# Gate rows of the modulation: stored as one contiguous row per token group, read back in 2 KB packets

## The chip, the cores and the metric

The kernel runs on one core of a Trainium2 chip. The metric is the device time of one execution in microseconds (us). Instructions are named by engine: PE (matrix products), DVE (vector), ACT (activations), POOL (gathers by index) and SP (issues DMAs only). ACT and POOL issue DMAs too.

## The reference, cut to what matters

Two token groups, P (128 context tokens) and S (256 noisy tokens), go through the same two layers. Each group has one conditioning vector, and each layer turns it into six rows of 1024 numbers:

```python
mod = jax.nn.silu(cvec) @ p['ada_w'][l] + p['ada_b'][l]
sh1, sc1, g1, sh2, sc2, g2 = jnp.split(mod[:, None, :], ADA_CHUNKS, axis=-1)
h = rms_norm(x, p['norm1_g'][l]) * (1.0 + sc1) + sh1
mix, kv = token_mixers(h, ...)
x = x + g1 * mix
h = rms_norm(x, p['norm2_g'][l]) * (1.0 + sc2) + sh2
x = x + g2 * peer_ffn(h, ...)
```

`token_mixers` is one input projection, three kinds of mixing and one output projection; `peer_ffn` picks experts by their keys out of 16384 and sums them. The gates g1 and g2 are the same for all tokens of a group: each multiplies a [tokens, 1024] result, so it has to stand in every one of the 128 partitions.

## The kernel before, in words

Each layer has two stages. `chain` does everything up to the choice of experts, for P and S interleaved; its tasks stand in a list with due times, and a scheduler then sets each engine's order with a timing model of its own, so one changed instruction can move others. `experts` follows. P's experts are gathered row by row (256 per layer, POOL issues, DVE multiplies: the tiles `ugt`, `vgt` and `pacc`). S goes densely over all 16384 experts in 128 steps c: SP loads a table block of 512 KB (`raw`), ACT and DVE split it in two (`hi`, `lo`), PE multiplies (`pP`), ACT and DVE make weights (`W`, `whl`), PE sums (`acc`). There are four `raw` buffers, and SP issues its DMAs strictly in order.

The six rows are made in twelve pieces of 512 columns by `ada_chunk`: PE multiplies four weight loads (`w`) into four 32-row groups of the bank `pada`, DVE adds the bias, and the tile `row` then holds, in partition 32q + r, columns 128q to 128q + 127 of group r (r = 0 is P, r = 1 is S; the other 30 rows of each 32 carry nothing). Shifts and scales are transposed on PE. Gates (`which` 2 and 5) go to HBM, into `grow`: SP stores the whole `row` tile, 128 rows of 512 bytes, once for each piece, eight times in all: four for layer 0 and four for layer 1, all of them while layer 0's `chain` runs (L200).

The gate comes back through `gate_half`: ACT issues a DMA that reads the group's four 512-byte rows of one half, 16 KB apart in `grow`, and writes them to all 128 partitions. All partitions read the same four rows. There are sixteen such reads: eight into `wo`, one for each half, group and layer, just before the output projection's result is multiplied by g1 (`wout`), and eight into two free `G` tiles in the dense loop (`finish`, c = FIN), where ACT first loads x of the group, then the two halves of g2.

The profile gives one line, L82, to everything that PE, DVE, ACT and POOL do, since a helper records it; so the rows are told apart by tile. SP's DMAs keep their lines: L314 loads `w`, L1014 loads `raw`, L200 stores `grow`.

Of the kernel before, what the change touches and what calls it, by code (L numbers as in the profile page):

```python
# [9 lines left out]
F32 = mybir.dt.float32  # L10
# [9 lines left out]
D = 1024  # L20
# [78 lines left out]
def trunk_kernel(ctx, tc, xin, silu_c, wts, adab, ccol, crow, finalg, rope, ohc, io2, skt,  # L99
                 sgut, lkT, lv, ut, ug, vg, y, ck_d, cv_d, ck_g, cv_g):  # L100
    nc = tc.nc
    V, A, TE, SY, GP = nc.vector, nc.scalar, nc.tensor, nc.sync, nc.gpsimd
# [6 lines left out]
    dpool = ctx.enter_context(tc.tile_pool(name="dpool", bufs=2, space=bass.MemoryType.DRAM))  # L109

    V, TE, A, GP = Follow(V), Follow(TE), Follow(A), Follow(GP)
# [3 lines left out]
    def bank(name, st=None):  # L115
        if st is not None and name + st.name in cur["tags"]:
            name += st.name
        tag, n = cur["tags"][name]
        return cur["psum"].tile([128, 512], F32, tag=tag, name=name, bufs=n)
# [45 lines left out]
    def transposes(cols, st=None):  # L165
        pt = bank("pt", st)
        for i, c in enumerate(cols):
            TE.transpose(pt[:, i * 128:(i + 1) * 128], c, ident)
        return pt
# [4 lines left out]
    def new_layer(l):  # L174
        L = Layer()
        L.l, L.have = l, set()
        L.lam_init = 0.8 - 0.6 * math.exp(-0.3 * l)
        L.modT = sp.tile([128, 4, KC, 2], F32, name="modT")
        L.cc = sp.tile([128, 20], F32, name="cc")
        A.dma_start(L.cc, ccol[l])  # L180
        L.grow = dpool.tile([2, 2, 128, 128], F32, name="grow")
        return L

    def ada_chunk(L, j, pieces):
        which, half = divmod(j, 2)
        L.have.add(j)
        ab = sm.tile([128, 128], F32, name="ab", bufs=2)
        A.dma_start(ab, adab[L.l, j])
        ps = bank("pada")
        k = 0  # L190
        for w in pieces:
            for kk in range(w.shape[1]):
                for q in range(4):
                    TE.matmul(ps[32 * q:32 * q + 32, 0:128], sT[:, k, :], w[:, kk, q * 128:(q + 1) * 128],
                              start=(k == 0), stop=(k == KC - 1), tile_position=(0, 32 * q))
                k += 1
        row = sm.tile([128, 128], F32, name="row", bufs=2)
        V.tensor_tensor(row, ps[:, 0:128], ab, op=ALU.add)
        if which in (2, 5):
            SY.dma_start(L.grow[which // 3, half], row)  # L200
            return
        pt = transposes([row])
        pv = pt[:, 0:128].rearrange("p (q r) -> p q r", r=32)[:, :, 0:2]
        m = {0: 0, 1: 1, 3: 2, 4: 3}[which]
        dst = L.modT[:, m, half * 4:(half + 1) * 4, :]
        if m % 2:
            g = L.cc[:, (m // 2) * 8 + half * 4:(m // 2) * 8 + half * 4 + 4]
            V.scalar_tensor_tensor(dst, pv, 1.0, g[:, :, None].to_broadcast([128, 4, 2]), op0=ALU.add, op1=ALU.mult)
        else:
            V.tensor_copy(dst, pv)  # L210

    def gate_half(L, which, half, row, gb):
        src = L.grow[which, half].rearrange("(q r) c -> q r c", r=32)[:, row, :]
        A.dma_start(gb.rearrange("p (q c) -> p q c", q=4), src[None].to_broadcast([128, 4, 128]))

    def gate_rows(L, which, row, gb):
        src = L.grow[which].rearrange("h (q r) c -> h q r c", r=32)[:, :, row, :]
        A.dma_start(gb.rearrange("p (h q c) -> p h q c", h=2, q=4), src[None].to_broadcast([128, 2, 4, 128]))


    class Retrieval:
# [64 lines left out]
    def chain(L, early_ada, Ln, R0):  # L286
        l = L.l
        with ExitStack() as es:
# [78 lines left out]
            def ada(M, js, cost, free=12):  # L367
                for j in js:
                    while j >= free and not cur["queried"]:
                        yield 3  # L370

                    ada_chunk(M, j, kpieces(j, P, M.l, S if M.l == 0 and j in (1, 3) else P))
                    yield cost
# [263 lines left out]
            def wout(st, blocks):  # L637
                for b in blocks:
                    load_x(st, b)
                yield from need(4, 5)  # L640
                for half in range(2):
                    hs = slice(half * 512, (half + 1) * 512)
                    pss = mm_tok(16 + half, [(st.mixT, b) for b in blocks], st)
                    g = s512(st, "wo")
                    gate_half(L, 0, half, st.row, g)
                    yield CW * st.nb
                    for b, ps in zip(blocks, pss):
                        t = s512(st, "wo")
                        V.tensor_tensor(t, ps, g, op=ALU.mult)
                        V.tensor_tensor(st.xs[b][:, hs], st.xs[b][:, hs], t, op=ALU.add)  # L650
                for b in blocks:
                    xd = dpool.tile([128, D], F32, name=f"x1{st.name}{b}")
                    SY.dma_start(xd, st.xs[b])
                    st.x[b] = xd
# [177 lines left out]
            def head(st):  # L832
                if not st.past and R0 is not None and LEFT:
                    while R0.n < NSLOT + R0.LAG:
                        yield 1.0
                    for half in range(2):
                        hs = slice(half * 512, (half + 1) * 512)
                        gb = s512(st, "gb")
                        gate_half(R0.L, 1, half, st.row, gb)
                        V.tensor_tensor(gb, R0.acc[:, hs], gb, op=ALU.mult)  # L840
                        V.tensor_tensor(st.xs[0][:, hs], st.xs[0][:, hs], gb, op=ALU.add)
                    xd = dpool.tile([128, D], F32, name="x2p")
                    SY.dma_start(xd, st.xs[0])
                    st.x[0] = xd
                elif st.next:
                    st.xs, st.next = st.next, {}
                else:
                    st.xs = {}
                    for b in range(st.nb):
                        load_x(st, b)  # L850
                if not st.past:
                    alloc_mix(st)
                    if st.hT is not None:
                        return
                hp = pp if st.past else tp
                st.hT = hp.tile([128, KC, st.T], F32, name=f"hT{st.name}")
                yield from normed_T(st, 0, st.hT, range(st.nb))
# [139 lines left out]
    def experts(L, R, Ln):  # L997
        l = L.l
        last = l == DEPTH - 1
        with ExitStack() as es:  # L1000
# [161 lines left out]
            def finish(c):  # L1162
                late_p = not last and LEFT
                if c == FIN[l]:
                    sp, sq = (g_tile(i).rearrange("p a t -> p (a t)").rearrange("p (n d) -> p n d", d=D) for i in (8, 9))
                    for i, n in enumerate(("xs0", "xs1", "gs")):
                        fin[n] = [sq[:, i, hs] for hs in halves]
                    fin["xp0"] = [sp[:, 0, hs] for hs in halves]
                    fin["gp"] = [sp[:, 1, hs] for hs in halves]
                    fin["fg"], fin["out"] = sp[:, 2], [sp[:, 3], sp[:, 0]]  # L1170
                    for st in (P, S):
                        if st is P and late_p:
                            continue
                        for b in range(st.nb):
                            for hs, t in zip(halves, fin[f"x{st.name}{b}"]):
                                A.dma_start(t, st.x[b][:, hs])
                        for half, t in enumerate(fin["g" + st.name]):
                            gate_half(L, 1, half, st.row, t)
                    if last:
                        A.dma_start(fin["fg"], finalg.to_broadcast([128, D]))  # L1180
# [66 lines left out]
            dense_loop()  # L1247

    L, R = new_layer(0), None
    for l in range(DEPTH):  # L1250
        Ln = new_layer(l + 1) if l + 1 < DEPTH else None
        R = chain(L, l == 0, Ln, R)
        R.L = L
        experts(L, R, Ln)
        L = Ln
# [86 lines left out]
```

## Time and profile before

| | |
|---|---|
| three runs | 2392.46, 2394.32, 2396.28 us; median 2394.32 |
| profiled execution | 2388.71 us, span 2386.9 us, granted PE clock 0.968 |
| busy share of the span | PE 93%, DVE 78%, ACT 37%, POOL 32% |
| DMA | 681.25 MB in 201998 packets, mean 285 GB/s |
| gate stores | 8, from 116.3 to 487.2 us |
| gate reads into `wo` | 8, from 128.6 to 1478.9 us |
| gate reads into `G` | 8, from 863.1 to 2094.9 us |

Layer 0's `chain` ends near 487 us and its dense loop near 1238 us; layer 1's end near 1622 and 2371 us. The share of busy time is an average over these four stretches. What one DMA costs has to be read in the few microseconds around it: who waits there, and how busy the 16 DMA engines are. A row of a stretch ("windows") gives busy time and instructions by engine, then the granted PE clock, the mean busy share of the 16 DMA engines and GB/s.

### The profile page before, as it was taken

The numbers are of one execution on the slowest core, as the hardware profiler recorded it, in microseconds if no ns is written. First come the engines' busy times: TensorE is split into PE (matmuls) and PEld (weight loads), VectorE is DVE, ScalarE is ACT, GpSimd is POOL, SyncE is SP. The second block draws the span as 40 slices with busy tenths as digits, with TensorE's granted clock in tenths as the row PEclk, the third lists the DMA queues.
The fourth block names the chain that finished last, engine by engine and source line by source line (L and its number), as shares of the span: only waits on it lengthen the run. The fifth ranks groups of instructions, "written<-read, shape, count | busy, mean of one in ns | idle before, by whom it ended". The sixth has DMA issues, their size and how long they took to land.

```text
span 2386.9 us, 38803 instructions
## 1 busy us (share of the span) xinstructions
PE 2218.8 (93%) x14466; PEld 1726.2 (72%) x14466; DVE 1860.0 (78%) x3795; ACT 894.4 (37%) x1848; POOL 755.0 (32%) x558
## 2 busy tenths in 40 slices
PE   6999879889999989999999998797999999999997
PEld 4446537676898768899974464586689877889996
DVE  1234668987999959899962466899889996999996
ACT  2224311143444334444442343114344343444443
POOL 0000043103544425455400002400345443545540
PEclk9998989999999999999999999899999999999999
DMA  8665699738998869999976424942899887999994
GB/s 331 211 221 175 215 356 360 275 111 293 369 376 319 287 224 400 366 375 383 367 257 203 130 89 147 356 138 90 291 356 388 336 285 260 394 386 383 380 374 161
DMA packets 201998, 681.25 MB, mean 285 GB/s; under 512 B 22225, under 2 KB 37201, under 8 KB 201809
## 3 DMA queue, kind: packets, MB, share of 16 engines
q1 hardware_dynamic: 112448, 397.66, 45.8%
q0 software_dynamic: 74160, 270.04, 30.7%
q10 hardware_dynamic: 15200, 11.07, 1.9%
q8 instruction: 114, 1.87, 0.3%
q14 instruction: 76, 0.61, 0.1%
HBM read 671.08 MB, written 7.60 MB: 284 GB/s over the span
## 4 chain that ended last, share of the span: by engine, by line
PE 71%; DVE 15%; DMA 9%; ACT 2%; issue 2%; ACTq 0%; POOL 0%; DVEq 0%; SPq 0%; POOLq 0%
PE acc L82 27%; PE pP L82 23%; PE mm L82 10%; DMA raw<-in_vg 3%; DMA w<-in_wts 3%; PE pt L82 3%; PE sc L82 2%; PE pG L82 2%; DVE ugt L82 2%; DVE si L82 2%; DVE pacc L82 2%; DVE lo L82 2%; DMA ugt<-in_ug,ei 1%; PE pq L82 1%; PE pg L82 1%
## 5 line engine op out<-in xcount | busy, mean ns | idle before, releaser
L82 POOL DMA_INDIRECT ugt<-in_ug,ei x256 | 360.8, 1409 | 975.9 <-DVE ugt L82 811.7
L82 DVE TENSOR_TENSOR lo<-raw,hi 128x1024 fp32r<-128x1024 f32 x418 | 504.9, 1220 | 108.5 <-ACT hi L82 90.4
L82 ACT ACTIVATE hi<-raw 128x1024 fp32r<-128x1024 f32 x418 | 435.6, 1057 | 343.4 <-DMA raw<-in_vg 179.4
L82 PE MATMUL acc<-hi,whl 128*128 128x512 f32 x1680 | 479.5, 400 | 19.3 <-ACT whl L82 11.2
L82 PE MATMUL pP<-hh,lo 128*128 128x256 f32 x1664 | 465.9, 280 | 8.8 <-DVE lo L82 8.7
L82 PE MATMUL pP<-hh,hi 128*128 128x256 f32 x1664 | 469.1, 282 | 1.5 <-ACT hi L82 1.5
L82 PE MATMUL pP<-hl,hi 128*128 128x256 f32 x1664 | 463.1, 278 | 0.0
L82 POOL DMA_INDIRECT vgt<-in_vg,ei x256 | 362.5, 1416 | 167.7 <-DVE pacc L82 73.2
L82 PEld LDWEIGHTS acc<-hi,whl 128*128 128x128 f32 x1680 | 313.2, 191 | 88.4 <-ACT whl L82 11.8
L82 DVE SCALAR_TENSOR_TENSOR ugt<-ugt,h 128x1024 f32<-128x1024 f32 x256 | 311.7, 1218 | 28.6 <-DMA ugt<-in_ug,ei 26.9
L82 DVE SCALAR_TENSOR_TENSOR pacc<-vgt,gz,pacc 128x1024 f32<-128x1024 f32 x254 | 324.9, 1279 | 3.9 <-DMA vgt<-in_vg,ei 3.5
L82 PEld LDWEIGHTS pP<-hh,lo 128*128 128x128 f32 x1664 | 312.6, 188 | 19.4 <-DVE lo L82 12.1
L82 PEld LDWEIGHTS pP<-hh,hi 128*128 128x128 f32 x1664 | 314.4, 189 | 10.3 <-issue 3.3
L82 PEld LDWEIGHTS pP<-hl,hi 128*128 128x128 f32 x1664 | 312.7, 188 | 3.0 <-issue 0.5
L82 PE MATMUL acc<-lo,whl 128*128 128x512 f32 x840 | 264.4, 398 | 0.1
L82 PEld LDWEIGHTS acc<-lo,whl 128*128 128x128 f32 x840 | 155.8, 191 | 31.5 <-DVE lo L82 0.7
L82 ACT ACTIVATE W<-pP 128x512 f32<-128x512 f32 x104 | 62.1, 597 | 300.0 <-PE pP L82 249.6
L82 POOL TENSOR_TENSOR rstd<-rstd,mhalf 128x1 f32<-128x1 f32 (+3 forms) x34 | 29.1, 861 | 434.1 <-DVE rstd L82 434.1
L82 ACT ACTIVATE G<-pG 128x128 f32<-128x128 f32 x512 | 94.4, 301 | 76.5 <-PE pG L82 75.5
L82 PE MATMUL mm<-w,hTs 128*128 128x512 f32 x256 | 117.6, 610 | 1.9 <-DMA w<-in_wts 1.8
L82 DVE TENSOR_TENSOR o<-ohio,i12d 128x2048 f16<-128x2048 f16 (+1 forms) x128 | 117.9, 952 | 0.8 <-DMA ohio<-in_io 0.7
L82 PE MATMUL mm<-hTs,w 128*128 128x256 f32 x512 | 117.9, 387 | 0.0
(248 smaller groups left out, 2716.2 us busy)
## 6 DMA issues: line engine op xcount, KB each, us to landing
raw<-in_vg SPq DMA_DIRECT2D x256, 512.0 KB
w<-in_wts SPq DMA_DIRECT2D x224, 512.0 KB
raw<-in_ut SPq DMA_DIRECT2D x224, 512.0 KB
w<-in_ut SPq DMA_DIRECT2D x32, 512.0 KB
ugt<-in_ug,ei POOLq DMA_INDIRECT x256
vgt<-in_vg,ei POOLq DMA_INDIRECT x256
x<-in_xin SPq DMA_DIRECT2D x5, 512.0 KB
wo<-grow ACTq DMA_DIRECT2D x8, 256.0 KB
```

What stands on the lines that cost most here:

```text
L82: self.last = f(*a, **k)
```

## The change

`grow` becomes one row of 1024 numbers for each gate and group. Each piece is stored by two DMAs, one for each group, that take four rows of 512 bytes each out of `row` and put them side by side. A half of a gate is then one piece of 2 KB, and a read is 128 packets of 2 KB where it was 512 packets of 512 bytes; it writes the same 256 KB. `gate_rows`, which nothing called, goes.

```diff
-        L.grow = dpool.tile([2, 2, 128, 128], F32, name="grow")
+        L.grow = dpool.tile([2, 2, D], F32, name="grow")
...
         if which in (2, 5):
-            SY.dma_start(L.grow[which // 3, half], row)
+            for r in range(2):
+                SY.dma_start(L.grow[which // 3, r, half * 512:half * 512 + 512].rearrange("(q c) -> q c", q=4),
+                             row.rearrange("(q r) c -> q r c", r=32)[:, r, :])
             return
...
     def gate_half(L, which, half, row, gb):
-        src = L.grow[which, half].rearrange("(q r) c -> q r c", r=32)[:, row, :]
-        A.dma_start(gb.rearrange("p (q c) -> p q c", q=4), src[None].to_broadcast([128, 4, 128]))
-
-    def gate_rows(L, which, row, gb):
-        src = L.grow[which].rearrange("h (q r) c -> h q r c", r=32)[:, :, row, :]
-        A.dma_start(gb.rearrange("p (h q c) -> p h q c", h=2, q=4), src[None].to_broadcast([128, 2, 4, 128]))
+        src = L.grow[which, row:row + 1, half * 512:half * 512 + 512]
+        A.dma_start(gb, src.to_broadcast([128, 512]))
```

The engines' instructions are the same in kind and number but for SP's eight more stores. The scheduler moves some near the end of layer 0's `chain`. On SP, at the end of that stage, before (the last `w` loads, a gate store, the small table `ohio` that the dense loop starts with, the first `raw` loads, the last gate store):

```order
L314 DMA w<-in_wts 128x1024 x5
L200 DMA grow<-row 128x128
L1004 DMA ohio<-in_io 128x128
L1014 DMA raw<-in_ut 128x1024 x4
L200 DMA grow<-row 128x128
```

The same place now:

```order
L312 DMA w<-in_wts 128x1024 x6
L201 DMA grow<-row 4x128 x2
L1002 DMA ohio<-in_io 128x128
L1012 DMA raw<-in_ut 128x1024 x4
L201 DMA grow<-row 4x128 x2
```

One more store stands ahead of `ohio`, and one more `w` load ahead of the store.

On PE at the same place, before (`pt<-ident,eo` turns S's chosen experts round for the dense loop, once for each block of 128 tokens, twice a block; `mm<-hTs,w` and `pada` are work for the dense loop and for layer 1 that fills gaps):

```order
L82 MATMUL pada<-w,sT 32x128 x13
L82 MATMUL pt<-ident,eo 128x128
L82 MATMUL pada<-w,sT 32x128 x11
L82 MATMUL mm<-hTs,w 128x256 x10
L82 MATMUL pada<-w,sT 32x128
L82 MATMUL pt<-ident,eo 128x128
L82 MATMUL pt<-ident,gate 128x128
```

And now:

```order
L82 MATMUL pada<-w,sT 32x128 x14
L82 MATMUL pt<-ident,eo 128x128
L82 MATMUL pada<-w,sT 32x128 x2
L82 MATMUL mm<-hTs,w 128x256 x3
L82 MATMUL pada<-w,sT 32x128 x8
L82 MATMUL mm<-hTs,w 128x256 x3
L82 MATMUL pada<-w,sT 32x128 x2
L82 MATMUL pt<-ident,eo 128x128
L82 MATMUL pt<-ident,gate 128x128
```

Between the last two `eo` transposes stood ten `mm` products and now stand six; the other four come after.

## The prediction

> **What bounds the kernel.** I read the page first, for the share of the engines and of the chain that ended last, then the DMA queues.
>
> ```profile
> span 2386.9 us, 38803 instructions
> PE 71%; DVE 15%; DMA 9%; ACT 2%; issue 2%; ACTq 0%; POOL 0%; DVEq 0%; SPq 0%; POOLq 0%
> q10 hardware_dynamic: 15200, 11.07, 1.9%
> L82 ACTq DMA_DIRECT2D wo<-grow x8: 366/384/1355, 128.6 to 1478.9; - x8
> L82 ACTq DMA_DIRECT2D G<-grow x8: 377/575/976, 863.1 to 2094.9; - x8
> ```
>
> PE bounds most of the span, and DMA holds 9% of the chain, some 215 us. ACT's own queue (q10), on which all sixteen gate reads run, keeps the DMA engines busy for 1.9% of the span. By the averages the change touches nothing. The last two rows (issue time, minimum/median/maximum in ns) say where the reads are, so I took the stretch around each of them. Here is one that runs almost alone, then the only other read of one row into all partitions that does (the parameter row `cr`, packets of 2304 bytes, at the start of layer 1), then a plain load (`ab`, 512-byte packets, a different address in every partition):
>
> ```profile
> DMA packets 422, 0.21 MB, mean 43 GB/s; under 512 B 3, under 2 KB 422, under 8 KB 422
> q10 hardware_dynamic: 422, 0.21, 27.7%
> ```
>
> ```profile
> DMA packets 35, 0.08 MB, mean 115 GB/s; under 512 B 0, under 2 KB 0, under 8 KB 35
> q10 hardware_dynamic: 35, 0.08, 28.8%
> ```
>
> ```profile
> DMA packets 136, 0.06 MB, mean 155 GB/s; under 512 B 15, under 2 KB 136, under 8 KB 136
> ```
>
> The stretches are 1336 to 1341, 1235.5 to 1236.2 and 467.4 to 467.8 us. A gate read gets 422 packets through in 5 us, 84 a microsecond and 43 GB/s, with the engines busy 28% of the time: nothing else competes, and still 512 packets need 6.1 us. The plain load moves packets of the same size at 155 GB/s. So it isn't the engines that are slow, it is reading the same few rows again and again. With longer packets from one row, `cr` gets 115 GB/s.
>
> What that does to others stands in the windows around the reads that fall among weight loads or gathers:
>
> ```profile
> 132.00:138.00 6.00, 6.00 (x69) 3.42 (x67) 2.35 (x12) 1.43 (x4) 0.70 (x1) 1.00 0.45 102
> 181.00:187.00 6.00, 6.00 (x15) 2.65 (x15) 2.29 (x4) 0.00 (x0) 0.00 (x0) 1.00 0.75 65
> 238.00:245.00 7.00, 6.13 (x55) 4.92 (x54) 4.33 (x25) 2.44 (x7) 1.01 (x1) 1.00 0.38 91
> 319.00:332.00 13.00, 11.34 (x57) 4.17 (x56) 10.40 (x19) 0.20 (x1) 6.61 (x6) 1.00 1.03 375
> 865.00:879.00 14.00, 12.50 (x64) 8.46 (x63) 1.24 (x2) 0.35 (x1) 0.00 (x0) 1.00 0.42 109
> 968.00:988.00 20.00, 18.46 (x110) 15.77 (x109) 16.71 (x21) 9.24 (x12) 9.72 (x7) 1.00 0.99 349
> 1480.00:1488.00 8.00, 8.00 (x20) 3.42 (x18) 4.92 (x8) 0.00 (x0) 5.23 (x5) 1.00 0.42 108
> 2006.00:2012.00 6.00, 6.00 (x20) 2.99 (x18) 2.42 (x2) 1.06 (x1) 0.00 (x0) 1.00 0.65 156
> 2100.00:2104.00 4.00, 4.00 (x37) 3.96 (x36) 3.66 (x5) 1.14 (x2) 1.80 (x2) 1.00 0.90 297
> ```
>
> The last column should be near 400 where loads are waiting (375 at 319); it falls to 65 to 109. All queues crawl while a gate read is under way. The chain of waits (start, us, what) carries a load there each time (the row at 467 is for later), and the timeline (start, us, engine, instruction, in brackets the idle time before it and who ended it) shows PE or DVE idle behind it:
>
> ```profile
> 130.11 11.03 DMA w<-in_wts
> 187.91 7.22 DMA w<-in_wts
> 237.34 10.46 DMA w<-in_wts
> 467.11 4.22 DVE eq L82 x9
> 865.04 14.79 DMA raw<-in_vg
> 1484.97 15.35 DMA ugt<-in_ug,ei
> 2007.22 8.84 DMA raw<-in_vg
> 2100.51 12.40 DMA raw<-in_vg
> ```
>
> ```profile
> 141.28 8.80 PE L82 MATMUL mm<-w,hTs 128*128 128x512 f32 x16 [1.82 <-DMA w<-in_wts]
> 191.45 0.64 PE L82 MATMUL pada<-w,sT 128*32 128x128 f32 x16 [3.57 <-DMA w<-in_wts]
> 247.85 1.08 PE L82 MATMUL pada<-w,sT 128*32 128x128 f32 x16 [3.72 <-DMA w<-in_wts]
> 877.22 0.28 PE L82 MATMUL pP<-hl,hi 128*128 128x256 f32 x1
> 882.19 0.58 ACT L82 ACTIVATE W<-pP 128x512 f32<-128x512 f32 x1
> 884.72 1.22 PE L82 MATMUL acc<-hi,whl 128*128 128x512 f32 x2 [7.22 <-ACT whl L82]
> 2020.94 1.22 PE L82 MATMUL acc<-hi,whl 128*128 128x512 f32 x2 [3.83 <-ACT whl L82]
> 1489.69 1.23 DVE L82 SCALAR_TENSOR_TENSOR ugt<-ugt,h 128x1024 f32<-128x1024 f32 x1 [4.70 <-DMA ugt<-in_ug,ei]
> ```
>
> **What a 2 KB read costs.** No row shows it. From below: if the packet is what counts, 128 packets at 84 a microsecond take 1.5 us. From above: if bytes from one place count, 256 KB at 43 GB/s take 6.1 us as before. I take `cr`'s 115 GB/s, 2.3 us, because its packets are nearest in size and also read by all partitions. A read then blocks the queues 3.8 us less, a pair 7.6 us.
>
> **The sum, stall by stall.** Every gain is capped by the idle time that PE or DVE has there.
> - 128.6 us: PE idles 1.82, so 1.8. 179.4: 3.57 at 191 and more in the products just after it, so the whole 3.8. 236.6: capped at 3.7.
> - 316.2: the engines are full (1.03), so only the packets' own time counts. 27.7% of 16 engines for 5 us over 422 packets is 53 ns a packet, 1.7 us for 512 packets spread over 16 engines; `cr` had 28.8% for 0.7 us over 35, 92 ns, 0.7 us for 128. The difference, 1.0, contains waiting and lies on no engine's path as such: 0 to 1.0, I take 0.2.
> - 863 (two reads): the `raw` load lands 7.6 earlier, but the products ahead of it keep PE until 877.5, and from the start of W on ACT to `acc` it is 2.5 (882.19 to 884.72); 884.7 becomes 880.0, gain 4.7. 962 (two): engines at 0.99, so 0.5 of 0 to 2.0.
> - 1335, 1374, 1424: as at 1336, no other load is in flight, nobody waits: 0. These three could be worth something only if the gate itself were late for DVE.
> - 1478.9: at a share of 0.42 the eight us lose 4.6 us of DMA time, the new read 1.6 (2.3 us at 0.28); the gathers are asked for a little late, so 2.5.
> - 2000 (two): PE idles 3.83, of which 2.5 are again the steps from W on: 1.3. 2094 (two): share 0.90, and ACT's issues (up to 976 ns) stand ahead of the next `hi`: 1.5.
>
> That makes 20.0. How much of it stays? SP issues a load when a buffer comes free, so what is late behind a stall is late by as much, and shifts with it; but between 342 and 472 us most pieces of the chain are DVE's (the one at 467 is the longest), and DVE also limits the loop from 885 to 1000. I keep 0.8: 16.0 (0.6 and 1 are the ends, 12.0 and 20.0).
>
> **The stores and the moved instructions.** SP issues eight DMAs more, and DVE's first step of the dense loop waits behind two of them:
>
> ```profile
> L200 SPq DMA_DIRECT2D grow<-row x8: 320/403/692, 116.3 to 487.2; - x8
> 474.01 5.78 PE L82 MATMUL mm<-hTs,w 128*128 128x256 f32 x20
> 480.54 0.42 DVE L82 CAST i<-pt 128x256 f16<-128x256 f32 x1 [5.42 <-PE pt L82]
> 481.97 4.71 DMA ohio<-in_io
> ```
>
> One store more ahead of `ohio`: +0.4 (403 ns), and the one after it delays `raw` loads that have four buffers. The others fall between `w` loads; if SP finds its buffers taken, as it mostly does there, they cost nothing, and 7 times 0.4 is their most. A store's 8 packets for 128 of the same size can only shorten it. On PE, ten `mm` products (twenty passes, 5.78 us) stood between the two `eo` transposes while DVE idled 5.42 for them; six stand there now, so 4 times 0.58: 2.3 less. The other moved rows are fillers under DVE's chain: 0, up to 2 either way.
>
> Sum: 16.0 + 2.3 - 0.4 = 17.9. The profiled execution took 2388.71 us (span 2386.9), which gives 2370.8; the median of the runs, 2394.32, is 5.6 above that execution, so I forecast 2376 for the median.
>
> **The rivals.**
> - Nothing happens to the reads. The Trainium skill, "DMA: Bandwidth & Descriptors", section Specifications, gives 512 bytes as the smallest transfer at line rate; by it packets of 512 bytes are long enough and 2 KB buys nothing. The trace at 1336 doesn't bear the rule out for a row that everyone reads (43 GB/s), but the same would follow if one place in HBM yields 43 GB/s at any packet size. Then 16 reads at 6.1 us remain, and 2.3 - 0.4 is all: 2392. Against it stands `cr`, an input at another place. Chance 0.15.
> - The reads get short, but DVE takes the time back: the first three gains (9.3) vanish between 342 and 472, that at 863 (4.7) in the loop up to 1000. 6.0 + 1.9 are left: 2386. For it: DVE is busy for 16.71 of the 20 us at 968; against it: for 1.24 of the 14 at 865, behind the load. Chance 0.15.
> - Slower, through SP: six of the eight second stores wait, in the new program, for an earlier DMA's semaphore. If that DMA is a `w` load still in flight, SP stands and so do all loads behind. The longest such wait so far is 3.4 us:
>
> ```profile
> SPq L314 <- DMA w<-in_wts: 21.1, 10, 3.4
> ```
>
>  Four stores before 270 us at 3.4 + 0.4 make 15.2; with unshortened reads, less 2.3, the result is 2407. From 5 us a store it would outweigh even the gain. Chance 0.07.
>
> **How the numbers follow.** The forecast has 0.63, at 2364 to 2383 by itself (2364: reads of 1.5 us, every stall's idle time gone and all kept; 2383: little more than half kept and no gain from the moved products). A change of 0.2%, 4.8 us, is about the least that a measurement of this kernel tells from none. Faster is the forecast and the second rival, less a little: 0.77; within 0.2% 0.16; slower 0.07. The range, 2362 to 2392, leaves out the SP rival and the far side of the first one.
>
> **What would show it.** Right: the read at 1336 takes 2 to 3 us from first to last packet, at 90 to 170 GB/s; the windows above no longer fall under 150 GB/s for 6 us; the loads at 130, 237 and 865 are 3 to 8 us shorter; DVE's wait of 5.42 is near 3. The first rival: that read still moves 43 GB/s. The second: the stalls are gone and DVE's gaps between 342 and 472 or at 885 to 1000 are wider. The third: SP waits for DMAs just ahead of L201. The forecast is wrong if a stall had a second cause behind the read, such as loads that SP issued late.

## The result and the profile after

The changed kernel takes 2358.76 us (median of 4 runs, 2354.8 to 2361.86), the kernel before, run beside it, 2395.03 (2392.46 to 2396.28). The ratio is 0.9849, 95% interval 0.9832 to 0.9866. The gain is 36.3 us between medians; 2376 was forecast, and the range ended at 2362. The profiled execution took 2361.86 us, 26.9 less than the one of before. One execution of `only_wo` below ran at a granted clock of 0.744 and took 2815 us; its ratio leaves it out. From the page of the profile after, the span, the chain that ended last, and ACT's own queue:

```profile
span 2360.1 us, 38816 instructions
PE 72%; DVE 14%; DMA 7%; issue 3%; ACT 2%; POOL 1%; ACTq 0%; POOLq 0%; DVEq 0%; SPq 0%
q10 hardware_dynamic: 9056, 11.07, 1.5%
```

DMA's share of the chain fell from 9% to 7% (in a second profile of each, from 12% to 6%), and q10 moves the same bytes in 6144 packets fewer (16 reads by 384). The same kernel's windows, at the places of six of the nine rows of before (busy time and instructions by engine, clock, DMA share, GB/s):

```profile
131.50:137.50 6.00, 6.00 (x69) 3.43 (x67) 2.36 (x13) 1.43 (x4) 0.70 (x1) 1.00 1.00 332
177.00:183.00 6.00, 6.00 (x14) 2.65 (x15) 2.44 (x5) 0.00 (x0) 0.00 (x0) 1.00 0.58 170
228.50:235.50 7.00, 7.00 (x74) 5.89 (x74) 4.24 (x24) 2.44 (x7) 1.01 (x1) 1.00 0.73 218
851.00:865.00 14.00, 14.00 (x72) 9.87 (x71) 8.63 (x12) 5.84 (x8) 3.16 (x3) 1.00 0.75 256
1455.50:1463.50 8.00, 8.00 (x20) 3.56 (x19) 6.88 (x11) 0.00 (x0) 5.86 (x5) 1.00 0.96 326
1984.00:1990.00 6.00, 6.00 (x19) 2.89 (x18) 1.57 (x2) 1.37 (x2) 0.00 (x0) 1.00 0.88 313
```

Where before the last column fell to 65 to 156, it now stays at 170 or above; at the other three places it was 297 to 375 and is 404 to 408. The read that runs alone, now at 1309.6 (the DMA view of 1310.6 to 1312.4):

```profile
DMA packets 135, 0.26 MB, mean 142 GB/s; under 512 B 13, under 2 KB 13, under 8 KB 134
q10 hardware_dynamic: 134, 0.25, 57.1%
```

From its first packet to its last it takes 2.0 us where it took 6.2. All of that looks like the forecast. The reason given for it, longer packets, was wrong, as the next runs show.

### The profile page after: what moved, and what is told of

The parts are those of the page before. It is cut to its first block, busy times and chain, and to the rows that moved or that the text cites. A ratio compares the mean times of both kernels' runs of the same rounds, so it can differ in the third digit from the quotient of the medians.

```text
span 2360.1 us, 38816 instructions
## 1 busy us (share of the span) xinstructions
PE 2211.2 (94%) x14466; PEld 1722.7 (73%) x14466; DVE 1861.4 (79%) x3795; ACT 890.6 (38%) x1848; POOL 754.2 (32%) x558
## 4 chain that ended last, share of the span: by engine, by line
PE 72%; DVE 14%; DMA 7%; issue 3%; ACT 2%; POOL 1%; ACTq 0%; POOLq 0%; DVEq 0%; SPq 0%
PE acc L82 27%; PE pP L82 24%; PE mm L82 9%; PE pt L82 3%; DMA ugt<-in_ug,ei 2%; PE pq L82 2%; DMA w<-in_wts 2%; PE pG L82 2%; DVE ugt L82 2%; DMA raw<-in_vg 2%; PE sc L82 2%; DVE pacc L82 1%; PE pada L82 1%; DVE si L82 1%; DVE lo L82 1%
```

## The experiments

Each run's ratio is against the kernel before on the same chip.

### Which part of the change does it: the packets, or the stores and the moved instructions?

`reads_512` is the changed kernel with short packets, with the same instructions in the same order on every engine:

```diff
-L.grow = dpool.tile([2, 2, D], ...)
+L.grow = dpool.tile([2, 2, 8, 256], ...)          # pieces of 512 bytes, 1 KB apart
-SY.dma_start(L.grow[which // 3, r, half * 512:half * 512 + 512].rearrange(...), ...)
+SY.dma_start(L.grow[which // 3, r, half * 4:half * 4 + 4, 0:128], ...)
-src = L.grow[which, row:row + 1, half * 512:half * 512 + 512]
+src = L.grow[which, row, half * 4:half * 4 + 4, 0:128]      # 4 packets of 512 bytes
...
```

> The changed kernel, but a gate read is again 512 packets of 512 bytes (the four pieces of a row lie 1 KB apart in HBM). The two stores, and the order of the instructions on every engine, are those of the changed kernel. Theory A (the packets' length is the whole change): nothing is left of the gain, 2395 us within 5, and the read that runs alone near 1310 takes 6 us. Rival B (about half of the 36 us comes from the moved instructions and the stores, since my sum for the reads was 16): 2377.

Measured: 2358.31 us, ratio 0.9857 (0.9836 to 0.9878). Both theories missed. The long packets are worth nothing: with 512 packets of 512 bytes, 1 KB apart instead of 16 KB, the lone read (window 1308.5 to 1310.4) runs as fast as with 2 KB.

```profile
DMA packets 517, 0.27 MB, mean 140 GB/s; under 512 B 14, under 2 KB 516, under 8 KB 516
q10 hardware_dynamic: 516, 0.26, 46.0%
```

`reads_2k_only` is the other half: before's order, one store of 128 rows a piece, and 2 KB reads. Against the kernel before (the read, left out here, is that of the changed kernel):

```diff
-L.grow = dpool.tile([2, 2, 128, 128], ...)
+L.grow = dpool.tile([2, 32, D], ...)
-SY.dma_start(L.grow[which // 3, half], row)
+SY.dma_start(L.grow[which // 3, :, half * 512:half * 512 + 512].rearrange("r (q c) -> q r c", q=4), row)
...
```

> The kernel before, with its one store of 128 rows a piece and its order on every engine, but the store puts a group's pieces side by side, so that a read is 128 packets of 2 KB. Theory A: the whole gain, 2359 us within 5. Rival B: only the reads' part, 2377. If A holds here and in the run with short packets, the two stores and the moved instructions are worth less than 5 us together.

Measured: 2360.22 us, 0.9855 (0.983 to 0.988). The whole gain comes without the second stores and without any moved instruction: together these are worth nothing that can be told from zero.

`reads_spread` keeps the stores, the order and the packets' number and length of before, but lets each partition read a stored row of its own, four times; the rows lie 512 bytes apart:

```diff
-src = L.grow[which, half].rearrange("(q r) c -> q r c", r=32)[:, row, :]     # 4 rows for all
+src = L.grow[which, half]                                # row p for partition p, four times
...
```

> The kernel before, same order, same stores, same 512 packets of 512 bytes in a read, but each partition reads one row of its own of the 128 stored ones, four times (so the gate's values are others). Theory C (one row that everyone reads is slow): the read alone takes about 256 KB / 155 GB/s = 1.7 us, and the time is that of the changed kernel or a little less, 2350 to 2362. Rival D (the number of packets is what costs): 6 us, and 2395 as before.

Measured: 2360.43 us, 0.9862 (0.9842 to 0.9882); theory C holds. The same 512 packets, alone at 1308.2 to 1309.2:

```profile
DMA packets 509, 0.25 MB, mean 253 GB/s; under 512 B 15, under 2 KB 509, under 8 KB 509
```

So it is neither the length nor the number of packets, it is where they read. And a read of 1.1 to 1.4 us makes the kernel no faster, as far as these intervals tell, than one of 2.0.

### How far apart may the pieces lie?

Two kernels of DMAs only. The first:

> A kernel of DMAs only; it computes nothing of the reference. Reads of 128 partitions from HBM on ACT's queue, one after the other, from 1, 4, 16 and 128 different rows and in packets of 512 bytes to 4 KB; first alone, twice, then under a stream of 512 KB loads that SP issues. Theory C: the time goes by packets that hit the same row, about 64 to 84 a microsecond: 4 rows with 512 packets 6 us, 1 row with 512 packets 6 us or more, 1 KB packets 3 to 4 us, 2 KB 2 us, 4 KB from one row about 2 to 3 us though it is twice the bytes; 16 and 128 rows near 200 GB/s or more, 1.3 us for 256 KB. Rival D: 512 packets take 6 us from 128 rows too, and 128 packets 2 us from any number of rows. Under the stream: with one row the loads fall below 150 GB/s for as long as the read takes; with 128 rows they stay over 300.

Its windows, each from a read's first packet to its last (the last column is GB/s): four times the same 512 bytes; 128 rows, 4 KB apart, in 512-byte packets; one, 16 and 128 rows in 2 KB packets; one row in 4 KB packets.

```profile
55.48:61.99 6.51, 0.00 (x0) 0.00 (x0) 1.00 0.21 40
63.40:65.29 1.89, 0.00 (x0) 0.00 (x0) 1.00 0.48 138
70.35:72.10 1.75, 0.00 (x0) 0.00 (x0) 1.00 0.45 150
78.38:79.53 1.15, 0.00 (x0) 0.00 (x0) 1.00 0.62 228
81.16:82.45 1.29, 0.00 (x0) 0.00 (x0) 1.00 0.63 203
84.04:86.08 2.04, 0.00 (x0) 0.00 (x0) 1.00 0.67 255
```

One place of 512 bytes gives 40 GB/s, a row of 2 KB 150, a row of 4 KB 255. Rival D is out: 512 packets from 128 rows take 1.89 us. Theory C holds in kind but not in all: the four rows 128 KB apart took 3.0 and 3.9 us instead of 6. Nor do the bytes that a read spreads over set the rate alone: 128 rows 4 KB apart give 138 in 512-byte packets and 203 in 2 KB ones, where 16 rows give 228, and four rows of 2 KB, not shown, gave 86 to 96. The part under a stream of loads says nothing, since SP's loads waited for the reads there (SP's waits: total, times, longest):

```profile
SPq L54 <- DMA gb<-h: 118.3, 7, 70.1
```

The second scans the distance, from three starts:

> A kernel of DMAs only; it computes nothing of the reference. 128 partitions read 256 KB each time from HBM: one place of 512 bytes, 1 KB, 2 KB again and again, then four pieces of 512 bytes at distances from 640 bytes to 128 KB; all from three different starts. Theory E: 41 GB/s for one place of 512 bytes, about 80 for 1 KB, 130 to 150 for 2 KB; four pieces give 120 to 150 at most distances, and 42 at 16 KB and at some of its multiples, at every start. Rival F: the rate falls with the distance, and is low at all of 8 KB and more.

The third start: one place of 512 bytes, 1 KB, 2 KB; then four pieces of 512 bytes at 640 bytes, 1, 2, 4, 8, 16, 20, 32, 64 and 128 KB from each other.

```profile
144.98:151.37 6.39, 0.00 (x0) 0.00 (x0) 1.00 0.22 41
152.70:155.80 3.10, 0.00 (x0) 0.00 (x0) 1.00 0.36 84
157.08:158.83 1.75, 0.00 (x0) 0.00 (x0) 1.00 0.44 149
160.23:162.02 1.79, 0.00 (x0) 0.00 (x0) 1.00 0.53 146
163.40:165.21 1.81, 0.00 (x0) 0.00 (x0) 1.00 0.49 145
166.56:168.31 1.75, 0.00 (x0) 0.00 (x0) 1.00 0.52 150
169.66:173.29 3.63, 0.00 (x0) 0.00 (x0) 1.00 0.45 72
174.68:180.57 5.89, 0.00 (x0) 0.00 (x0) 1.00 0.25 44
182.10:188.01 5.91, 0.00 (x0) 0.00 (x0) 1.00 0.25 44
189.35:192.45 3.10, 0.00 (x0) 0.00 (x0) 1.00 0.35 85
193.80:199.69 5.89, 0.00 (x0) 0.00 (x0) 1.00 0.19 45
201.12:205.61 4.49, 0.00 (x0) 0.00 (x0) 1.00 0.32 58
206.98:210.02 3.04, 0.00 (x0) 0.00 (x0) 1.00 0.36 86
```

The three starts agree within a fifth. 41, 84, 149: about 40 GB/s for each place of 512 bytes that the pieces cover. Up to 2 KB apart four pieces lie in four places, 4 and 20 KB apart in two, 8, 16 and 32 KB apart in one. That reads as a period of 8 KB; at 64 and 128 KB it doesn't fit (58 and 86 where it says 44), so it isn't the whole address rule. Theory E holds for 16 KB and misses 4, 8 and 20 KB; rival F is wrong, since 20 KB is faster than 8 and 16.

`pitch_20k` and `pitch_16k5` put that into the kernel before, with one number changed:

```diff
-L.grow = dpool.tile([2, 2, 128, 128], ...)
+L.grow = dpool.tile([2, 2, 128, 160], ...)[:, :, :, 0:128]     # pitch_20k
+L.grow = dpool.tile([2, 2, 128, 132], ...)[:, :, :, 0:128]     # pitch_16k5
```

> The kernel before with one number changed: a stored row of grow takes 640 bytes of room, so the four pieces of a group lie 20 KB apart instead of 16 KB. Packets, stores and order on all engines are those of before. Theory E (rows 16 KB apart fall into one place of HBM, which yields 42 GB/s, and other distances don't): the read alone takes about 2 us, and the whole gain comes, 2360 us within 5. Rival F (pieces must lie near each other, within a KB or so): the read stays near 6 us, 2393. Rival G (there are few places, and 20 KB hits two of them): 3 to 4 us for the read, 2368 to 2380.

> The kernel before with one number changed: a stored row of grow takes 528 bytes of room instead of 512, so the four pieces of a group lie 16.5 KB apart instead of 16 KB. Packets, stores and order are those of before. If places repeat every 8 KB and are 512 bytes long (as the scan of distances reads: 2 KB apart 150 GB/s, 4 KB apart 72, 8 and 16 KB apart 44), the pieces now fall 0, 512, 1024 and 1536 bytes into that period, four places: the read alone takes 1.8 to 2.2 us, the load behind the pair at 863 is waited for 5 us instead of 14.6, and the time is 2359 within 5. If distances over 16 KB are bad as such, the time is 2370, as at 20 KB, or more.

20 KB: 2369.95 us, 0.9900 (0.9886 to 0.9914), rival G's number. 16.5 KB: 2362.08 us, 0.9856 (0.9817 to 0.9894), the whole gain from sixteen bytes a row. The three reads that run alone take 1.8 to 3.4 us in the first and 1.9 to 2.6, a little over the 1.8 to 2.2 expected, in the second. One stall shows the dose: ACT's first wait for the `raw` load behind the read pair in layer 0's loop, on ACT's timeline (in brackets the idle time), in before, `pitch_20k`, `pitch_16k5`, `reads_512` and after:

```profile
879.94 1.06 ACT L82 ACTIVATE hi<-raw 128x1024 fp32r<-128x1024 f32 x1 [14.58 <-DMA raw<-in_vg]
```

```profile
859.24 1.06 ACT L82 ACTIVATE hi<-raw 128x1024 fp32r<-128x1024 f32 x1 [9.09 <-DMA raw<-in_vg]
```

```profile
855.03 1.06 ACT L82 ACTIVATE hi<-raw 128x1024 fp32r<-128x1024 f32 x1 [6.29 <-DMA raw<-in_vg]
```

```profile
853.38 1.06 ACT L82 ACTIVATE hi<-raw 128x1024 fp32r<-128x1024 f32 x1 [4.97 <-DMA raw<-in_vg]
```

```profile
855.81 1.06 ACT L82 ACTIVATE hi<-raw 128x1024 fp32r<-128x1024 f32 x1 [4.75 <-DMA raw<-in_vg]
```

### Does a slow read really hold up other queues?

`dma_block` has seven loads at once on one queue and one read on the other.

> A kernel of DMAs and small vector steps; it computes nothing of the reference. Twelve phases, six kinds twice: seven loads of 512 KB issued at once on SP's queue, and on ACT's queue no read, or one read of 256 KB into all partitions: four pieces of 512 bytes 16 KB apart, 4 KB apart, 1 KB apart, one piece of 2 KB, and 128 rows of 2 KB. Theory C (a read from one place starves the loads): a phase without a read moves 3.67 MB at about 410 GB/s, 9 us; with a read from 128 rows 0.64 us more, which is its bytes; with four pieces in one place 5 us more or above; 4 KB apart 2 to 3, 1 KB apart and 2 KB 1 to 2. Rival H (the slow read only waits by itself, and in the kernel it is the waits for its end that cost): the loads land as early with it as without, give or take 0.7 us.

Windows from the loads' first packet to their last, second round: no read; pieces 16, 4 and 1 KB apart; one piece of 2 KB; 128 rows.

```profile
90.17:100.89 10.72, 1.00 (x6) 0.00 (x0) 1.00 0.89 342
102.93:117.78 14.85, 1.00 (x6) 0.00 (x0) 1.00 0.77 265
120.10:132.61 12.51, 1.00 (x6) 0.00 (x0) 1.00 0.83 314
134.68:146.37 11.69, 1.00 (x6) 0.00 (x0) 1.00 0.91 336
148.47:160.28 11.81, 1.01 (x6) 0.00 (x0) 1.00 0.95 333
162.39:173.08 10.69, 1.00 (x6) 0.00 (x0) 1.00 0.97 368
```

The loads end 4.1 us later beside the read from one place (the slow read), 1.8 beside two places, 1.0 and 1.1 beside four, not at all beside 128 rows. Theory C holds in kind, a little below its numbers, and rival H is out: the read takes the time from the loads themselves. SP's timeline shows a part of it: handing a load to the queue takes SP 0.3 to 0.5 us mostly, but 3.47 once beside the slow read and 1.31 once beside two places. In the kernel before, SP's third `raw` load behind the read pair at 863 took 2.76 us to hand over, where after the change it took 0.33.

### Which reads carry the gain?

`only_wo` and `only_g` are `reads_2k_only` for one gate, with the other stored and read as before:

```diff
+if which // 3 == 0:      # only_wo; == 1 in only_g
+    ... store and read as in reads_2k_only
+else:
+    ... store and read as before
```

> The kernel before with its order, but only the gate of the mixers (the eight reads into wo) has its pieces side by side and 2 KB reads; the gate of the experts is as before. From the traces of before and after, stall by stall: up to 285 us 16.3, at 1479 4.7, so 21 gained, of which the loop may take back 4: 2372 to 2376. Rival, by the prediction's sum: 12.0 for these reads, times 0.8: 2383.

> The kernel before with its order, but only the gate of the experts (the eight reads into G) has its pieces side by side and 2 KB reads. From the traces of before and after: 9.9 at 863, 3.1 at 985, 4.4 at 2000, about 1.5 at 2094, so 19: 2374. Rival, by the prediction's sum: 8.0, times 0.8: 2387. If the two parts add, the gains of this run and of the one with wo alone make 33 to 36 together; if DVE takes gains back between the stages, they make more than the whole.

Ratios 0.9928 (0.9909 to 0.9947) and 0.9907 (0.989 to 0.9924), which is 17 us (13 to 22) and 22 us (18 to 26) of 2394. The two parts add up to the whole within their intervals. The forecasts from the traces, 2372 to 2376 and 2374, lie inside (2372 at the edge); those from the prediction's sum, 2383 and 2387, outside.

### Is there more to be had?

`one_read` is `reads_2k_only` with both halves of a gate in one read of 4 KB packets in the loop:

```diff
-for half, t in enumerate(fin["g" + st.name]):
-    gate_half(L, 1, half, st.row, t)
+A.dma_start(t, L.grow[1, st.row:st.row + 1, :].to_broadcast([128, D]))     # t: both halves
```

> The kernel with one store of 128 rows a piece and 2 KB reads, but in the loop the two halves of a gate are read at once, 128 packets of 4 KB: four reads instead of eight into G, and four issues of 0.5 us less on ACT. If reads still cost, each pair is about 1.6 us shorter (2.2 instead of 3.8 us) and the loop gains up to 6 us: 2353. If they have stopped to cost, as the run with every partition reading its own row says (1.3 us a read, and no faster than 2.0), 2359 within 4.

2356.72 us, 0.9845 (0.982 to 0.9871): no difference from the changed kernel that can be told. The interval, 2350 to 2363 us, holds both numbers expected, so this run doesn't decide whether the reads still cost; that they cost nothing that can be told rests on `reads_spread`.

### How much do two executions of one kernel differ?

> The kernel before once more, for a second profile. The profile that the prediction was made from took 2388.71 us, below all other executions seen by then. If that was chance, this one lies at 2390 to 2397, and the difference of 6 or so stands at the stalls behind gate reads if those scatter (the read pair at 863, the loads at 128, 179, 237), elsewhere if they don't.

> The changed kernel once more, for a second profile: 2355 to 2362. Held against the second profile of before, the difference is 32 to 38 us, where the first two profiles differ by 26.9.

2391.78 and 2363.74 us, 28.0 apart. The first lies where chance would put it; the second and the difference miss what was expected. The profiled pairs differ by 27 and 28, the medians by 36 and, over all runs of both here, by about 34. The first profile of before lies low among its kernel's runs and both of after lie high, by chance as far as the runs tell: a difference of two profiles is good to some 8 us here (36 less 28).

## Why the prediction was wrong, step by step

To size the stalls I compared starts of the same PE and DVE instructions, stretch by stretch, over all profiles: executions with slow reads at that place (before twice, and the part run that leaves it alone) against those with fast reads (after twice, `reads_512`, `reads_2k_only`, `reads_spread` and the other part run). The last row leaves out both part runs. The time of a stretch less that in the first execution of before, in us (negative is shorter), and the gain, slow less fast:

```
stretch     read          slow reads       fast reads         gain   forecast
                          mean (spread)    mean (spread)
 120- 150   128.6       -1.2 (-2.0..0.0)  -3.6 (-3.6..-3.6)   2.3     1.8
 150- 210   179.4       -1.9 (-4.3..0.0)  -2.9 (-3.6..-2.3)   1.0     3.8
 210- 285   236.6       -3.2 (-5.9..0.0)  -8.9 (-9.6..-6.7)   5.7     3.7
 285- 485   316.2       -0.4 (-1.7..0.4)  -0.4 (-1.9..0.6)   -0.1     0.2
 858- 895   863 pair    -0.2 (-0.8..0.3)  -9.6 (-9.6..-9.5)   9.4     4.7
 895- 995   962 pair     1.9 ( 0.0..2.9)  -0.3 (-1.4..0.3)    2.2     0.5
1230-1470   three alone  1.0 ( 0.0..2.9)   0.9 (-0.3..2.5)    0.1     0
1470-1490   1478.9       0.3 ( 0.0..0.6)  -3.2 (-3.6..-2.7)   3.5     2.5
1995-2090   2000 pair    0.1 (-0.2..0.4)  -3.9 (-5.4..-2.7)   4.0     1.3
2090-2160   2094 pair    2.6 ( 0.0..6.5)  -0.7 (-1.5..0.9)    3.3     1.5
1490-1560   (no read)    0.6 ( 0.0..1.2)   4.2 ( 1.0..5.5)   -3.6
```

The reads' stretches make 31.4 where 20.0 was forecast. The `wo` reads make 12.5, against 12.0, but that is luck: 2.8 too much at 179.4 stands against 2.0 too little at 236.6 and 1.0 at 1478.9. The loop's four pairs make 18.9, against 8.0. So in the forecast of 17.9 for the profile the loop's reads were 10.9 short, the factor 0.8 took 4.0 more, and the moved products less the store gave 1.9 that did not come.

- **The step that failed: "every gain is capped by the idle time that PE or DVE has there".** It priced the loop's four pairs at 8.0 us, and they gained 18.9; the forecast's best case, 2364, stood under the same cap. At 863 the 4.7 us that are missing are two things: 2.5 us of idle time were taken off without need (the next point), and 2.2 us are what idle time does to PE's clock, which the cap leaves out. At 2000, 2.7 are missing, and the same 2.5 are nearly all of it. At 962 and 2094 the forecast's 0.5 and 1.5 were choices; 2.2 and 3.3 came, and no run separates the causes there. For the clock, before, the windows behind the late product at 247.9, then just ahead of that at 884.7, from it on, and 4 us later (the clock is the third number from the end):

```profile
248.00:252.00 4.00, 4.00 (x38) 2.70 (x34) 1.85 (x12) 0.49 (x1) 0.00 (x0) 0.60 0.79 286
...
877.00:885.00 8.00, 0.78 (x6) 0.58 (x5) 3.28 (x5) 3.56 (x5) 1.15 (x1) 0.85 0.48 172
885.00:889.00 4.00, 4.00 (x10) 3.14 (x11) 4.00 (x7) 2.04 (x3) 1.89 (x2) 0.50 0.71 283
889.00:893.00 4.00, 4.00 (x19) 3.29 (x19) 4.00 (x5) 1.27 (x2) 3.69 (x2) 0.94 0.74 198
```

After, at 187 to 195 (behind the read at 175.6) and at the place of the last three rows:

```profile
191.00:195.00 4.00, 3.95 (x17) 3.46 (x18) 0.17 (x1) 1.58 (x3) 0.00 (x0) 0.50 1.02 411
...
851.00:860.00 9.00, 9.00 (x36) 5.18 (x35) 4.20 (x5) 2.75 (x5) 0.46 (x1) 1.00 0.74 239
860.00:864.00 4.00, 4.00 (x33) 3.89 (x32) 3.43 (x5) 2.08 (x3) 2.01 (x2) 1.00 0.91 344
```

After 7.22 us of idle time PE ran at half clock for 4 us: 0.50 of 4 us and 0.06 of 4 us are 2.2 lost, and 7.2 + 2.2 = 9.4 is what the place gained. At 248 before, the granted clock is 0.60 for the 4 us after an idle 3.72: 1.6 lost, 5.3 together, where 5.7 was gained (8.9 against this execution alone). Elsewhere the same working gives too much: at 141, 1.82 idle and 0.62 for 4 us make 3.3 for 2.3 gained; at 2021, 3.83 idle and 0.50 make 5.8 for 4.0 gained, and DVE is busy for 34.5 of the 35 us from 2025 on. So the sum of the two fits at 884.7 and, over the executions, at 248, but it is no general price. Behind the second read the clock falls in the changed kernel too (0.50, with the loads at full rate): PE still waits for weights there, three times for 1.1 to 1.4 us, and the place gained 1.0 instead of 3.8. The windows quoted in the prediction have the clock's column; they ended too early to show it. The rule stands in the Trainium skill, "TensorE: Matmul & The Clock Gate", section HAM oscillation — how this bites in real kernels: waits for DMA longer than a window of about 3.4 us send PE back to half its clock. The trace agrees for the waits of 3.72, 3.83 and 7.22 us, but the clock fell after shorter ones too, 1.82 us at 141 and the three of 1.1 to 1.4.
- **"From the start of W on ACT to `acc` it is 2.5"** was taken off at 863 and again at 2000. Before, W stood behind `hi` on ACT, and `hi` waited for the load until 879.94. After the change W starts at 858.09, while PE's products still run, and PE is busy for all of 851 to 864: the steps come earlier with the load, and nothing had to be taken off.
- **What a 2 KB read costs**: 2.3 us was forecast, 2.0 measured. That it came so near is partly luck: `cr` was taken for its long packets, and its 2304 bytes span four and a half places of 512 bytes where the new row spans four. **Why**: "reading the same few rows again and again" was right, "the packet is what counts" was not. The plain load that I held against it differed in address, not only in sharing. The Trainium skill, "DMA: Bandwidth & Descriptors", section Specifications, gives 512 bytes as the smallest transfer at line rate. I said that the trace doesn't bear it out; `reads_512` does, in that 512-byte packets read at 140 GB/s where 2 KB ones read at 142. The same page of the Trainium skill, section Latency and other measured facts, has tile copies with rows 2 to 8 MiB apart as slow and a pad of 4 KiB as the cure. Here, where all partitions read the same rows, 16 KB was slow already, and 512 bytes more between two pieces cured it.
- **0.8 kept**: in the stretches of DVE's chain, 285 to 485 and 895 to 995, nothing was given back, so the second rival fell where it was placed. About 3.6 us went back between 1490 and 1560, where I had not placed it, but not for the fast read at 1478.9: `only_g`, where that read is slow, takes 4.2 us longer there too, `pitch_20k` 0.6 and `reads_512` 1.0. In the profile of after, DVE waits 3.75 us there for a gathered row (`ugt`) and PE 5.73 behind DVE; in that of before DVE's longest such wait past 1490 is 2.16.
- **The moved products, -2.3, and the store, +0.4**: nothing. `i<-pt` on DVE's timeline after, which should have waited near 3, still waits 5.15:

```profile
463.12 0.42 DVE L82 CAST i<-pt 128x256 f16<-128x256 f32 x1 [5.15 <-PE pt L82]
```

  PE's timeline there has the products now in two groups:

```profile
456.35 2.93 PE L82 MATMUL mm<-hTs,w 128*128 128x256 f32 x6
459.21 1.08 PE L82 MATMUL pada<-w,sT 128*32 128x128 f32 x16
460.22 2.15 PE L82 MATMUL mm<-hTs,w 128*128 128x256 f32 x6
```

  Twelve passes take 5.08 us where twenty took 5.78: 0.49 and 0.36 us a pass instead of 0.29, behind 2.71 us in which PE waited. In `reads_2k_only`, in before's order, the wait is 3.78, so one execution decides little here.

- **The third rival**: SP did wait at the new stores, on the `w` loads as named, but in two cases and for 2.3 us at most (below: total, times, longest), and with one store instead of two the time is the same.

```profile
SPq L201 <- DMA w<-in_wts: 4.6, 2, 2.3
```

- **The first rival** was nearer to the cause than the forecast: one place does yield 43 GB/s. It fell because 2 KB side by side are four places.
- **From the profile to the median**: 5.6 was added to a sum made against one execution. The forecast for the profile was 2370.8, 8.9 above the one that came; executions of before differ by 6 us in the stretch 210 to 285 alone, so a sum over single gaps of one profile carries that.

What isn't settled: why that gathered row is waited for longer in most of the faster executions, what the pairs at 962 and 2094 gained by, and how addresses map to places beyond 32 KB.

## What to carry to other kernels

When many partitions read the same few rows, look at the distance of the rows in HBM before the length of the packets: here 8, 16 or 32 KB put four pieces in one place, and sixteen bytes of padding a row gave the same gain as the rewritten layout. Such a read costs more than its bytes, because loads on other queues wait with it. And when you price a stall of PE, look at the slow clock after it besides its idle time, take nothing off for steps that move with the load, and size it from more than one execution.

## What the runs showed of the hardware

One place of 512 bytes of HBM, read by all partitions, gives about 40 GB/s (35 to 45) with nothing else under way, two give 71 to 86, four 124 to 151, 2 KB rows at 16 addresses 222 to 229. Four pieces 64 KB apart give 58 and 128 KB apart 81 to 89, which the period of 8 KB doesn't explain. Packets of 512 bytes reach 253 GB/s from 128 neighbouring rows. A read of 256 KB from one place holds back 3.67 MB of loads on another queue by 4.1 us, one from four places by 1.0 to 1.1. Beside the first, SP took 3.47 us to hand over a load that takes it 0.3 to 0.5 mostly. At four places where PE had waited 1.8 to 7.2 us, its granted clock was 0.50 to 0.62 over the next 4 us.
